# All of the down projection with the activations held in the array, the last norm in [tokens, columns], and shorter waits in the residual's turns

## The chip, the cores and the metric

The kernel runs on one core of one Trainium2 chip. The metric is the device time of one execution in microseconds (us); a kernel's time is the median of its runs. Three runs of the kernel before took 2245.82, 2247.30 and 2247.95 us.

## The reference

A decoder trunk in float32: 256 tokens, model width 2048, two layers (0 and 1). What it computes, cut to what matters here:

```python
for l in range(2):
    z = rmsnorm(x, attn_norm[l]) @ w_in[l]              # 2048 -> 4 head groups x (q, k, v) of 512
    x = x + concat(fox, moba, diff, stick_breaking)(z) @ w_out[l]
    h = rmsnorm(x, ffn_norm[l])
    act = silu(h @ w_gate[l]) * (h @ w_up[l])            # 2048 -> 5632
    x = x + act @ w_down[l]                              # 5632 -> 2048
return rmsnorm(x, final_norm)
# rmsnorm(x, g) = x / sqrt(mean(x * x over the 2048 columns) + 1e-6) * g
```

## The kernel before

**Number format.** Every weight is split on the chip into a rounded high half and the rest, a low half (hi and lo); activations are split in the same way. A product is the sum of three matmuls: hi by hi, hi by lo and lo by hi.

**Weights.** They come as blocks of 128 x 1024 float32 (512 KB) in the order of `plan()`. `run_ahead(b)` (L226) stands ahead of block b's matmuls: it issues the loads on SP's queue up to block b+5 (four raw buffers) and splits block b+2. Of a split, ACT makes hi (L199) and DVE makes lo (L200), into three pairs of buffers, so the split of block b+2 can't start before TensorE is through with block b-1. A load waits until its raw buffer's former block is split.

**Two forms of product.** `rows_block` (L360) holds the activations in the array (128 tokens) and streams 512 weight columns: 12 matmuls of 512 columns for a block, and the result is [tokens, columns]. `gate_up_product` (L377) does the same for gate and up. `product` (L414) holds the weights and streams the activations, so that the result is [columns, tokens]: for a block 8 matmuls of 512 columns and 8 of 256 (L431, L432), or, with `split_halves=False`, 24 matmuls of 256 columns (L435 to L437).

**The residual** `x_all` lies as [columns, tokens], 16 tiles `xs[j]` of 128 x 256. A result of `rows_block` has to be turned before it is added. `turn_steps` (L394) does that: two DVE transposes of 32x32 squares (L399), one DMA to DRAM (`mem`, L402), four DMAs back (`back`, L408). `add_turned` (L895) then adds `back` to four of the tiles with one DVE instruction (L899), and for each of the four makes the next product's halves `xh` (ACT L303, DVE L304) and the square (ACT L298), which POOL sums (L299).

**The order of the work** is written out by hand, and every engine runs its instructions in that order. Evacuations are generators in a FIFO queue, `evacs`. After each block's matmuls `tick()` takes one step of the oldest generator; a `yield` ends a step. A residual's turn has seven steps: transposes; `mem`; nothing; `back`; nothing; the add with two tiles' halves; two tiles' halves. So five splits are in the engines' queues between the transposes and the add.

**Where turns are added to the residual.** The output projection makes four groups of 512 columns, n = 0 to 3, in `OUT_ORDER`: n = 0 and 1 end two blocks apart, n = 2 and 3 take eight blocks each. So several of these turns follow one another in the FIFO queue without a free step. The down projection makes groups n = 0 to 2 with `rows_block` (22 blocks each, one turn each) and the last 512 columns as two groups of 256 with `product` (11 blocks each). In layer 0 both have hi and lo streamed together and are added by `add_to_x` (L874) without a turn. In layer 1 the last group goes straight to `final_norm` (L974).

**The end.** `final_norm` adds the last two tiles, sums the squares over partitions with matmuls against ones (L981), makes 1/sqrt with one Newton step, spreads it over partitions with a diagonal matmul (L324), scales the 16 tiles on DVE (L1007) and POOL (L1012), and stores `y_t` (2 MB) with ten DMAs. The final norm's gain is multiplied into each tile earlier.

Of the kernel before, what the change touches and what calls it, by code (L numbers as in the profile page):

```python
# [11 lines left out]
F32 = mybir.dt.float32  # L12
# [3 lines left out]
ALU = mybir.AluOpType  # L16
# [85 lines left out]
V_FIN = DEPTH * V_LAYER  # L102
V_ALL = V_FIN + 16


def lay_out(inp):
# [15 lines left out]
    for l in range(DEPTH):  # L122
        w_in, every = inp["w_in"][l][pd], slice(None)
        v = vec[:, l * V_LAYER:(l + 1) * V_LAYER]
        v[:, V_GA:V_GA + 16] = inp["attn_norm"][l][pd].reshape(16, P).T
        v[:, V_GF:V_GF + 16] = inp["ffn_norm"][l][pd].reshape(16, P).T
        v[:, V_WF:V_WF + 64] = w_in[:, FG0:FG0 + NH].reshape(16, P, NH).transpose(1, 0, 2).reshape(P, 64)
        v[:, V_SUB] = inp["diff_subln"][l]
        v[:, V_B:V_B + NH] = inp["b_fgate"][l]
        for n, name in enumerate(("diff_lq1", "diff_lk1", "diff_lq2", "diff_lk2")):  # L130
            v[:, V_LAM + 64 * n:V_LAM + 64 * (n + 1)] = inp[name][l]
        for kind, what, nb in plan():
            if what[0] != l:
                continue
            if kind == "in":
                put(w_in, every, columns(*what[1:]), GC)
            elif kind == "out":
                order = np.concatenate([HEAD0[g] * P + np.arange(GW) for g in ORDER])
                put(inp["w_out"][l], order[what[2] * 256:what[2] * 256 + 256], np.arange(what[1] * GC, what[1] * GC + GC), GC)
            elif kind == "ffn":  # L140
                c = slice(what[1] * GC, what[1] * GC + GC)
                for n, name in enumerate(("w_gate", "w_up")):
                    blocks[at:at + NJ, :, n * GC:n * GC + GC] = inp[name][l][:, c][pd].reshape(NJ, P, GC)
                at += NJ
            elif kind == "down":
                put(inp["w_down"][l], pf, slice(what[1] * GC, what[1] * GC + GC), GC)
            else:
                put(inp["w_down"][l], pf, pd[what[1] * 256:what[1] * 256 + 256], 256)
    vec[:, V_FIN:V_FIN + 16] = inp["final_norm"][pd].reshape(16, P).T
    return {"x_t": x_t, "vec": vec, "w": blocks, "consts": constants()}  # L150
# [7 lines left out]
def plan():  # L158

    out = []  # L160
    for l in range(DEPTH):
# [4 lines left out]
        out += [("down", (l, c), NFC * 2) for c in range(3)]  # L166
        out += [("last", (l, c), NFC) for c in (6, 7)]
# [4 lines left out]
def trunk(ctx: ExitStack, tc: tile.TileContext, x_t, vec, w, consts, y_t):  # L172
# [72 lines left out]
    def cst(at, n=P):  # L245
        return con[:, at:at + n]
# [69 lines left out]
    def diag_product(cols):  # L316

        diag = tp.tile([P, 2, P], F32, name="diag", tag="g", bufs=1)
        for t in range(2):
            V.tensor_scalar(diag[:, t], ident, cols[:, t:t + 1], None, op0=ALU.mult)  # L320
        yield
        pbc = ps.tile([P, 512], F32, name="pbc", tag="at")
        for t in range(2):
            T.matmul(pbc[:, t * P:(t + 1) * P], cst(C_ONE), diag[:, t], start=t == 0, stop=t == 1)  # L324
        return pbc

# [67 lines left out]
    def turn_steps(get, back=None):  # L394
# [8 lines left out]
        yield  # L403
        yield
# [5 lines left out]
        yield  # L410
        yield
        return back.rearrange("p a k n -> p k a n")

    def product(sources, n_b, tags=("mm",), order=None, split_halves=True, done=None):  # L414


        nonlocal block
        outs = [None] * len(tags)
        for n, kb in order or [(n, kb) for kb in range(n_b) for n in range(len(tags))]:
            if kb == 0:  # L420
                outs[n] = [ps.tile([P, 2 * S], F32, name=f"po{c}", tag=tags[n]) for c in range(2)]
            run_ahead(block)
            hi, lo = halves.pop(block)
            for kk in range(4):
                k = kb * 4 + kk
                xk = sources(k)
                for c in range(2):
                    at = kk * 256 + c * P
                    end = k == 4 * n_b - 1
                    if split_halves:  # L430
                        T.matmul(outs[n][c], hi[:, at:at + P], xk, start=k == 0, stop=False)  # L431
                        T.matmul(outs[n][c][:, S:], lo[:, at:at + P], xk[:, :S], start=False, stop=end)  # L432
                    else:
                        o = outs[n][c][:, :S]
                        T.matmul(o, hi[:, at:at + P], xk[:, S:], start=k == 0, stop=False)  # L435
                        T.matmul(o, lo[:, at:at + P], xk[:, :S], start=False, stop=False)
                        T.matmul(o, hi[:, at:at + P], xk[:, :S], start=False, stop=end)  # L437
            block += 1
            if done and kb == n_b - 1:
                done(n, outs[n])  # L440
            tick()
        return outs
# [431 lines left out]
    def add_to_x(c, po, gain):  # L874


        def use(j):
            if gain is not None:
                halves_of_x(j, gain(j))
            square_sum(j)  # L880
            if gain is None:
                A.activation(xs[j], xs[j], AF.Copy, scale=vecs[:, V_FIN + j:V_FIN + j + 1])

        for i in range(2):
            j = 2 * c + i
            t = tp.tile([P, S], F32, name="xt", tag="sq")
            V.tensor_tensor(t, xs[j], po[i][:, S:], op=ALU.add)
            V.tensor_tensor(xs[j], t, po[i][:, :S], op=ALU.add)
            if i:
                use(j - 1)  # L890
            yield
        use(2 * c + 1)
        yield

    def add_turned(n, outs, gain):  # L895

        new = yield from turn_steps(lambda t: outs[t])
        of = x_all[:, 4 * n:4 * n + 4].rearrange("p k (a n) -> p k a n", n=32)
        V.tensor_tensor(of, of, new, op=ALU.add)  # L899
        for j in range(4 * n, 4 * n + 4):  # L900
            if gain is not None:
                halves_of_x(j, gain(j))
            square_sum(j)
            if gain is None:
                A.activation(xs[j], xs[j], AF.Copy, scale=vecs[:, V_FIN + j:V_FIN + j + 1])
            if j % 2:
                yield

# [19 lines left out]
    def ffn(l):  # L928
# [24 lines left out]

        evacs.append(norm_steps("mm"))
        for c in range(NFC):
            evacs.append(act_steps(c, *gate_up_product(("at", "mm")[c % 2])))
        new_norm()
        xh.clear()
        last = l + 1 == DEPTH
        gain = None if last else lambda j: vcol(l + 1, V_GA + j)  # L960
        for n in range(3):
# [3 lines left out]
            evacs.append(add_turned(n, outs, gain))  # L965
        if last:
            A.activation(tp.tile([P, 1], F32, name="pre", tag="pre", bufs=1), cst(C_ONE, 1), AF.Sqrt)
        evacs.append(add_to_x(6, product(source, 11)[0], gain))
        if last:
            final_norm(product(source, 11, split_halves=False)[0])  # L970
        else:
            evacs.append(add_to_x(7, product(source, 11)[0], gain))

    def final_norm(po):  # L974

        drain(evacs)
        sums = ps.tile([P, 2], F32, name="sums_ps", tag="at")

        def add(sq, first, last):
            for t in range(2):  # L980
                T.matmul(sums[:, t:t + 1], sq[:, t * P:(t + 1) * P], cst(C_ONE, 1), start=first and t == 0,  # L981
                         stop=last and t == 1)

        add(state["acc"], True, False)
        for i in range(2):
            j = NJ - 2 + i
            V.tensor_tensor(xs[j], xs[j], po[i][:, :S], op=ALU.add)
            sq = tp.tile([P, S], F32, name="sq", tag="sq")
            A.activation(sq, xs[j], AF.Square)
            add(sq, False, i == 1)  # L990
        v = tp.tile([P, 2], F32, name="v", tag="nv")
        V.tensor_scalar(v, sums, 1.0 / D, EPS, op0=ALU.mult, op1=ALU.add)
        r = tp.tile([P, 2, 2], F32, name="rf", tag="rf", bufs=1)
        A.activation(r[:, 0], v, AF.Sqrt)
        for j in range(NJ - 2, NJ):
            A.activation(xs[j], xs[j], AF.Copy, scale=vecs[:, V_FIN + j:V_FIN + j + 1])
# [4 lines left out]
        pbc = finish(diag_product(r[:, 0]))  # L1001
        rbc = tp.tile([P, S], F32, name="rbc", tag="gt", bufs=1)
        A.activation(rbc, pbc[:, :S], AF.Copy)
        at = 0
        for n in (1, 1, 2, 2, 2, 2, 1, 1):
            for j in range(at, at + n):
                V.tensor_tensor(xs[j], xs[j], pbc[:, :S], op=ALU.mult)  # L1007
            nc.sync.dma_start(y_t[:, at:at + n], x_all[:, at:at + n])
            at += n
        for j in range(at, NJ, 2):  # L1010
            for i in range(2):
                G.tensor_tensor(xs[j + i], xs[j + i], rbc, op=ALU.mult)  # L1012
            nc.scalar.dma_start(y_t[:, j:j + 2], x_all[:, j:j + 2])
# [31 lines left out]
```

## Time and profile before

| | |
|---|---|
| median of three runs | 2247.3 us |
| the profiled execution | 2250.89 us |
| its span, first to last instruction | 2249.1 us |
| TensorE busy | 2227.5 us, 99% of the span |
| DVE busy | 1300.6 us, 58% |
| ACT busy | 1056.8 us, 47% |
| bytes moved | 473.31 MB, mean 210 GB/s |
| granted TensorE clock | 0.998 of 2.4 GHz |

Matmuls overlap their neighbours, so a busy share of TensorE near 100% doesn't say that it runs at its peak: the distance between the starts of two matmuls counts. A matmul's own duration in the rows is longer than that distance. Where a row has brackets, they hold the engine's idle time before the instruction and what ended it.

### The profile page before, as it was taken

The numbers are of one execution on the slowest core, as the hardware profiler recorded it, in microseconds if no ns is written. First come the engines' busy times: TensorE is split into PE (matmuls) and PEld (weight loads), VectorE is DVE, ScalarE is ACT, GpSimd is POOL, SyncE is SP. The second block draws the span as 40 slices with busy tenths as digits, with TensorE's granted clock in tenths as the row PEclk, the third lists the DMA queues.
The fourth block names the chain that finished last, engine by engine and source line by source line (L and its number), as shares of the span: only waits on it lengthen the run. The fifth ranks groups of instructions, "written<-read, shape, count | busy, mean of one in ns | idle before, by whom it ended". The sixth has DMA issues, their size and how long they took to land.

```text
span 2249.1 us, 27206 instructions
## 1 busy us (share of the span) xinstructions
PE 2227.5 (99%) x10257; PEld 1845.3 (82%) x10257; DVE 1300.6 (58%) x1450; ACT 1056.8 (47%) x1306; POOL 213.8 (10%) x206
## 2 busy tenths in 40 slices
PE   9999999999999999999999999999999999999998
PEld 6888887788888888888888888887888888888887
DVE  6768655655555555455566776566555555554444
ACT  6455644544444444444444555445444444444443
POOL 2019101100000000000000380011000000000001
PEclk9999999999999999999999999999999999999999
DMA  7766566776667667666657566576666766766674
GB/s 267 223 197 208 179 194 199 233 225 219 211 221 224 210 213 230 210 208 208 199 195 235 183 197 200 165 236 223 219 212 222 223 211 214 228 214 206 212 217 131
DMA packets 187491, 473.31 MB, mean 210 GB/s; under 512 B 17248, under 2 KB 71264, under 8 KB 187360
## 3 DMA queue, kind: packets, MB, share of 16 engines
q1 hardware_dynamic: 186928, 471.05, 65.7%
q8 instruction: 80, 1.31, 0.2%
q10 hardware_dynamic: 432, 0.53, 0.1%
q14 instruction: 51, 0.42, 0.0%
HBM read 442.16 MB, written 29.36 MB: 210 GB/s over the span
## 4 chain that ended last, share of the span: by engine, by line
PE 89%; DMA 4%; DVE 3%; ACT 1%; issue 1%; SPq 1%; DVEq 0%; ACTq 0%
PE gate L389 20%; PE up L389 20%; PE po L371 7%; PE po L373 7%; PE po L372 7%; PE in L371 7%; PE in L372 7%; PE in L373 7%; PE po L431 3%; DMA back<-mem 2%; PE po L432 1%; DVE lo L200 1%; DMA mem<-tr 1%; ACT hi L199 1%; DMA raw<-w 1%
## 5 line engine op out<-in xcount | busy, mean ns | idle before, releaser
L200 DVE TENSOR_TENSOR lo<-raw,hi 128x1024 fp32r<-128x1024 f32 (+1 forms) x785 | 962.9, 1229 | 886.5 <-ACT hi L199 886.2
L199 ACT ACTIVATE hi<-raw 128x1024 fp32r<-128x1024 f32 (+1 forms) x785 | 829.9, 1059 | 1078.5 <-PE up L389 494.5
L389 PE MATMUL gate<-hi,xh 128*128 128x512 f32 x1408 | 548.4, 389 | 0.9 <-ACT hi L199 0.9
L389 PE MATMUL up<-hi,xh 128*128 128x512 f32 x1408 | 548.3, 389 | 0.0
L389 PEld LDWEIGHTS gate<-hi,xh 128*128 128x128 f32 x1408 | 264.5, 188 | 56.4 <-ACT hi L199 1.8
L389 PEld LDWEIGHTS up<-hi,xh 128*128 128x128 f32 x1408 | 264.3, 188 | 54.9
L371 PE MATMUL in<-hi,xh 128*128 128x512 f32 x768 | 303.4, 395 | 1.0 <-ACT hi L199 1.0
L372 PE MATMUL in<-lo,xh 128*128 128x512 f32 x768 | 300.0, 391 | 2.1 <-DVE lo L200 2.1
L373 PE MATMUL in<-hi,xh 128*128 128x512 f32 x768 | 299.5, 390 | 0.0
L389 PE MATMUL gate<-lo,xh 128*128 128x512 f32 x704 | 274.6, 390 | 1.1 <-DVE lo L200 1.1
L389 PE MATMUL up<-lo,xh 128*128 128x512 f32 x704 | 274.2, 389 | 0.0
L299 POOL TENSOR_TENSOR acc<-acc,sq 128x256 f32<-128x256 f32 x73 | 67.9, 930 | 1726.0 <-ACT sq L298 1723.2
L371 PE MATMUL po<-hi,act 128*128 128x512 f32 x528 | 205.5, 389 | 0.0
L373 PE MATMUL po<-hi,act 128*128 128x512 f32 x528 | 205.5, 389 | 0.0
L372 PE MATMUL po<-lo,act 128*128 128x512 f32 x528 | 205.5, 389 | 0.0
L372 PEld LDWEIGHTS in<-lo,xh 128*128 128x128 f32 x768 | 144.5, 188 | 33.3 <-DVE lo L200 4.6
L371 PEld LDWEIGHTS in<-hi,xh 128*128 128x128 f32 x768 | 144.4, 188 | 31.1 <-ACT hi L199 2.3
L373 PEld LDWEIGHTS in<-hi,xh 128*128 128x128 f32 x768 | 144.3, 188 | 30.4
L389 PEld LDWEIGHTS gate<-lo,xh 128*128 128x128 f32 x704 | 132.2, 188 | 30.3 <-DVE lo L200 3.2
L389 PEld LDWEIGHTS up<-lo,xh 128*128 128x128 f32 x704 | 132.1, 188 | 27.3
L373 PEld LDWEIGHTS po<-hi,act 128*128 128x128 f32 x528 | 99.1, 188 | 20.7
L372 PEld LDWEIGHTS po<-lo,act 128*128 128x128 f32 x528 | 99.1, 188 | 20.5
(218 smaller groups left out, 1920.7 us busy)
## 6 DMA issues: line engine op xcount, KB each, us to landing
raw<-w SPq DMA_DIRECT2D x783, 512.0 KB, 4.2
mem<-tr SPq DMA_DIRECT2D x52, 512.0 KB, 4.2
back<-mem SPq DMA_DIRECT2D x176, 128.0 KB, 5.2
k<-mem SPq DMA_DIRECT2D x24, 128.0 KB, 5.0
x_all<-x_t SPq DMA_DIRECT2D x7, 256.0 KB, 6.5
q<-mem SPq DMA_DIRECT2D x8, 128.0 KB, 3.9
y_t<-x_all SPq DMA_DIRECT2D x4, 256.0 KB, 3.0
raw<-w SPq DMA_DIRECT2D x2, 256.0 KB, 3.7
```

The lines of the kernel that those rows point to most:

```text
L199: A.activation(hi[:, c], raw[:, c], AF.Copy)
L200: V.tensor_tensor(lo[:, c], raw[:, c], hi[:, c].bitcast(F32), op=ALU.subtract)
L299: G.tensor_tensor(state["acc"], state["acc"], sq, op=ALU.add)
L371: T.matmul(outs[t], xlo, wh, start=first, stop=False)
L372: T.matmul(outs[t], xhi, wl, start=False, stop=False)
L373: T.matmul(outs[t], xhi, wh, start=False, stop=last)
L389: T.matmul(outs[n][t], st, wt[:, n * GC:(n + 1) * GC], start=first, stop=last)
L431: T.matmul(outs[n][c], hi[:, at:at + P], xk, start=k == 0, stop=False)
L432: T.matmul(outs[n][c][:, S:], lo[:, at:at + P], xk[:, :S], start=False, stop=end)
```

## The change

- `turn_steps` gets a parameter `wait`: the free steps after `mem` and again after `back`. It stays at 2 for the q, k and activation turns. `add_turned` passes 1, so a residual's turn has five steps: transposes; `mem`; `back`; the add with two tiles' halves; two tiles' halves.
- `down` has four groups of 512 columns, all with `rows_block`; `product` and `add_to_x` go. In layer 0 the fourth group is turned and added like the others, while layer 1's first input product runs.
- In layer 1 the residual is turned to [tokens, columns] once, ahead of down: `row_steps`, four of them, each after the activation turn of chunks 2 to 5 of gate and up. Down's four groups are then added without a turn (`last_steps`), squares are summed along the columns by ACT, and the final norm's gain comes as four tiles of 128 x 512 loaded from `fin`.
- `final_norm` has no matmuls; the result is stored as `y` [128, 2, 2048] with eight DMAs of 256 KB.

```diff
@@ plan
-        out += [("down", (l, c), NFC * 2) for c in range(3)]
-        out += [("last", (l, c), NFC) for c in (6, 7)]
+        out += [("down", (l, c), NFC * 2) for c in range(4)]
@@ turn_steps
-    def turn_steps(get, back=None):
+    def turn_steps(get, back=None, wait=2):
         ...
         nc.sync.dma_start(mem.rearrange("t i r g n -> (i r) t (g n)"), tr)
-        yield
-        yield
+        for _ in range(wait):
+            yield
         ...
         for g in range(4):
             nc.sync.dma_start(back[32 * g:32 * g + 32].rearrange("r a k n -> r a (k n)"),
                               mem[:, :, :, g].rearrange("t i r n -> r (t i) n"))
-        yield
-        yield
+        for _ in range(wait):
+            yield
         return back.rearrange("p a k n -> p k a n")
@@ add_turned
-        new = yield from turn_steps(lambda t: outs[t])
+        new = yield from turn_steps(lambda t: outs[t], wait=1)
@@ new
+    def row(n):
+        return x_all[:, 4 * n:4 * n + 4].rearrange("p k s -> p (k s)").rearrange("p (t c) -> p t c", t=2)
+
+    def row_steps(n):
+        c = tp.tile([P, 8, 4, 32], F32, name="c", tag="back", bufs=1)
+        A.activation(c, x_all[:, 4 * n:4 * n + 4].rearrange("p k (a n) -> p a k n", n=32), AF.Copy)
+        yield
+        tr = tp.tile([P, 8, P], F32, name="trb", tag="tr", bufs=1)
+        for t in range(2):
+            V.transpose(tr[:, 4 * t:4 * t + 4].rearrange("p a n -> p (a n)"),
+                        c[:, 4 * t:4 * t + 4].rearrange("p a k n -> p (a k n)"))
+        yield
+        mem = dr.tile([8, 32, 4, P], F32, name="memb", tag="mem")
+        for g in range(4):
+            nc.sync.dma_start(mem[:, :, g].rearrange("a c n -> c a n"), tr[32 * g:32 * g + 32])
+        yield
+        yield
+        nc.sync.dma_start(row(n), mem.rearrange("(t i) c g n -> (i c) t (g n)", t=2))
+        yield
@@ ffn
         for c in range(NFC):
             evacs.append(act_steps(c, *gate_up_product(("at", "mm")[c % 2])))
+            if last and 2 <= c < 6:
+                evacs.append(row_steps(c - 2))
         ...
-        for n in range(3):
+        for n in range(4):
             outs = [ps.tile([P, GC], F32, name=f"po{t}", tag="mm") for t in range(2)]
             for kb in range(NF // 2):
                 rows_block(source, outs, kb, NF // 2)
-            evacs.append(add_turned(n, outs, gain))
+                if last and kb == 4:
+                    gains[n] = big.tile([P, GC], F32, name=f"fin{n}", tag=f"xh{n}")
+                    nc.sync.dma_start(gains[n], fin[:, n * GC:n * GC + GC])
+            if not last:
+                evacs.append(add_turned(n, outs, lambda j: vcol(l + 1, V_GA + j)))
+            elif n < 3:
+                evacs.append(last_steps(n, outs, ssq, gains[n]))
         if last:
+            final_norm(outs, ssq, gains[3])
-            A.activation(tp.tile([P, 1], F32, name="pre", tag="pre", bufs=1), cst(C_ONE, 1), AF.Sqrt)
-        evacs.append(add_to_x(6, product(source, 11)[0], gain))
-        if last:
-            final_norm(product(source, 11, split_halves=False)[0])
-        else:
-            evacs.append(add_to_x(7, product(source, 11)[0], gain))
+    def last_steps(n, outs, ssq, gain):
+        x = row(n)
+        for t in range(2):
+            V.tensor_tensor(x[:, t], x[:, t], outs[t], op=ALU.add)
+        yield
+        junk = tp.tile([P, 2, GC], F32, name="junk", tag="tr", bufs=1)
+        for t in range(2):
+            A.activation(junk[:, t], x[:, t], AF.Square, accum_out=ssq[:, t, n:n + 1])
+        yield
+        V.tensor_tensor(x, x, gain[:, None, :].to_broadcast([P, 2, GC]), op=ALU.mult)
+        if n == 2:
+            A.activation(tp.tile([P, 1], F32, name="pre", tag="pre", bufs=1), cst(C_ONE, 1), AF.Sqrt)
+        yield
@@ final_norm (its new body)
+        drain(evacs)
+        x = row(3)
+        ...
+        for t in range(2):
+            V.tensor_tensor(x[:, t], x[:, t], outs[t], op=ALU.add)
+            A.activation(junk[:, t], x[:, t], AF.Square, accum_out=ssq[:, t, 3:4])
+        end = tp.tile([P, 2, GC], F32, name="end", tag="g", bufs=1)
+        V.tensor_tensor(end[:, 0], x[:, 0], gain, op=ALU.mult)
+        v = tp.tile([P, 2], F32, name="v", tag="nv")
+        V.tensor_reduce(v, ssq, axis=AX, op=ALU.add)
+        V.tensor_scalar(v, v, 1.0 / D, EPS, op0=ALU.mult, op1=ALU.add)
         ...
+        for n in range(4):
+            x = row(n) if n < 3 else end
+            for t in range(2):
+                to = y[:, t, n * GC:n * GC + GC]
+                if n == 3 and t == 1:
+                    V.scalar_tensor_tensor(end[:, t], row(3)[:, t], r[:, 0, t:t + 1], gain, op0=ALU.mult, op1=ALU.mult)
+                    nc.sync.dma_start(to, x[:, t])
+                elif t == 0 or n == 3:
+                    V.tensor_scalar(x[:, t], x[:, t], r[:, 0, t:t + 1], None, op0=ALU.mult)
+                    nc.sync.dma_start(to, x[:, t])
+                else:
+                    A.activation(x[:, t], x[:, t], AF.Copy, scale=r[:, 0, t:t + 1])
+                    nc.scalar.dma_start(to, x[:, t])
```

## Rows read from the trace of the kernel before

**Rows 1.** The page's part 1: engine, busy us (share of the span), instructions.

```profile
PE 2227.5 (99%) x10257; PEld 1845.3 (82%) x10257; DVE 1300.6 (58%) x1450; ACT 1056.8 (47%) x1306; POOL 213.8 (10%) x206
```

**Rows 2.** Windows: from:to length, then PE, PEld, DVE, ACT, POOL, clock, DMA.

```profile
1060.87:1123.04 62.17, 62.17 (x354) 53.96 (x352) 34.88 (x35) 27.46 (x34) 5.42 (x6) 1.00 0.64 203
1993.09:2172.61 179.52, 179.52 (x794) 148.72 (x792) 89.24 (x78) 79.92 (x88) 6.51 (x7) 1.00 0.66 211
2172.61:2203.69 31.08, 31.08 (x178) 26.97 (x176) 15.84 (x14) 14.77 (x20) 3.61 (x4) 1.00 0.74 218
2203.69:2235.37 31.68, 31.68 (x267) 31.68 (x266) 12.69 (x14) 11.16 (x13) 2.88 (x2) 1.00 0.32 104
2235.53:2249.10 13.57, 2.61 (x16) 2.15 (x15) 5.81 (x21) 2.22 (x6) 2.78 (x4) 0.62 0.43 155
```

**Rows 3.** Waits: who waited for whom, us in total, times, longest.

```profile
DVE x_all L899 <- DMA back<-mem: 12.0, 7, 2.6
...
SPq L408 <- DMA mem<-tr: 24.2, 29, 2.2
```

**Rows 4.** Timeline, DVE then SP, layer 0's first down turn (start, length).

```profile
943.63 1.31 DVE L399 STREAM_TRANSPOSE tr<-po 128x512 f32<-128x512 f32 x2
...
950.64 1.23 DVE L200 TENSOR_TENSOR lo<-raw,hi 128x1024 fp32r<-128x1024 f32 x1 [1.50 <-ACT hi L199]
...
957.23 1.22 DVE L899 TENSOR_TENSOR x_all<-x_all,back 128x1024 f32<-128x1024 f32 x1
...
944.96 0.38 SPq L402 DMA_DIRECT2D mem<-tr  x1
946.46 3.05 SPq L190 DMA_DIRECT2D raw<-w  x2
949.89 1.80 SPq L408 DMA_DIRECT2D back<-mem  x4
```

**Rows 5.** Timeline, DVE, output projection's turn n = 1 in layer 0.

```profile
373.27 1.30 DVE L399 STREAM_TRANSPOSE tr<-po 128x512 f32<-128x512 f32 x2
...
377.91 1.23 DVE L200 TENSOR_TENSOR lo<-raw,hi 128x1024 fp32r<-128x1024 f32 x1 [1.10 <-ACT hi L199]
...
387.05 1.23 DVE L899 TENSOR_TENSOR x_all<-x_all,back 128x1024 f32<-128x1024 f32 x1 [2.47 <-DMA back<-mem]
```

**Rows 6.** Timeline, DVE then PE, around turn n = 3's add.

```profile
414.40 1.30 DVE L399 STREAM_TRANSPOSE tr<-po 128x512 f32<-128x512 f32 x2
...
427.30 1.23 DVE L899 TENSOR_TENSOR x_all<-x_all,back 128x1024 f32<-128x1024 f32 x1 [2.36 <-DMA back<-mem]
...
430.35 0.39 PE L389 MATMUL up<-hi,xh 128*128 128x512 f32 x1
431.08 0.50 PE L389 MATMUL gate<-hi,xh 128*128 128x512 f32 x1 [0.34 <-ACT hi L199]
...
432.34 0.50 PE L389 MATMUL gate<-lo,xh 128*128 128x512 f32 x1 [0.53 <-DVE lo L200]
```

**Rows 7.** Source lines L402, then L408, all turns: issue of one DMA to landing.

```profile
DMA to landing us min/median/max: 3.4/4.2/6.8
...
DMA to landing us min/median/max: 3.1/5.1/7.4
```

**Rows 8.** Instructions by line: busy us, mean ns of one, idle before.

```profile
L943 ACT ACTIVATE act<-back 128x512 fp32r<-128x512 f32 x44 | 27.4, 622 | 12.4 <-DMA back<-mem 12.2
...
L543 DVE TENSOR_TENSOR mix<-po,mix 128x512 fp32r<-128x512 f32 x12 | 8.0, 678 | 1.1 <-ACT mix L542 1.1
```

**Rows 9.** The chain of waits at the end: start, length, what.

```profile
2238.24 0.17 DVE rf L1000
...
2240.45 0.42 DVE x_all L1007
```

**Rows 10.** DMA rate in 40 slices of the tail, 2235.5 to 2249.1.

```profile
GB/s 0 0 0 0 0 0 0 0 0 0 0 0 0 0 0 0 0 0 193 235 319 277 386 373 392 356 392 386 386 386 386 368 392 322 341 283 0 0 0 0
```

**Rows 11.** Window after the clock's fall at the end (columns as in rows 2).

```profile
2238.70:2249.10 10.40, 1.22 (x4) 0.93 (x4) 4.28 (x14) 0.38 (x1) 2.78 (x4) 0.50 0.56 202
```

More of the change, by code (lines that the diff above doesn't have):

```diff
@@ L101 @@
 V_LAYER = V_LAM + 4 * 64
-V_FIN = DEPTH * V_LAYER
-V_ALL = V_FIN + 16
+V_ALL = DEPTH * V_LAYER
 def lay_out(inp):
@@ L144, in lay_out @@
                 at += NJ
-            elif kind == "down":
+            else:
                 put(inp["w_down"][l], pf, slice(what[1] * GC, what[1] * GC + GC), GC)
-            else:
-                put(inp["w_down"][l], pf, pd[what[1] * 256:what[1] * 256 + 256], 256)
-    vec[:, V_FIN:V_FIN + 16] = inp["final_norm"][pd].reshape(16, P).T
-    return {"x_t": x_t, "vec": vec, "w": blocks, "consts": constants()}
+    fin = np.ascontiguousarray(np.broadcast_to(inp["final_norm"], (P, D)))
+    return {"x_t": x_t, "vec": vec, "w": blocks, "consts": constants(), "fin": fin}
 OUT_ORDER = [(c, kb) for c in range(2) for kb in range(6)] + [(c, kb) for c in range(2) for kb in range(6, 8)]
@@ L165, in plan, with trunk @@
         out += [("ffn", (l, c), NJ) for c in range(NFC)]
-        out += [("down", (l, c), NFC * 2) for c in range(3)]
-        out += [("last", (l, c), NFC) for c in (6, 7)]
+        out += [("down", (l, c), NFC * 2) for c in range(4)]
     return out
 @with_exitstack
-def trunk(ctx: ExitStack, tc: tile.TileContext, x_t, vec, w, consts, y_t):
+def trunk(ctx: ExitStack, tc: tile.TileContext, x_t, vec, w, consts, fin, y):
     nc = tc.nc
@@ L314, in inv_sqrt @@
         V.tensor_tensor(out, t[:, 0, :n], t[:, 1, :n], op=ALU.mult)
[L316 to L320, printed above, removed]
-        yield
[L322 to L325, printed above, removed]
     def norm_steps(tag="at"):
@@ L409, in turn_steps @@
                               mem[:, :, :, g].rearrange("t i r n -> r (t i) n"))
-        yield
-        yield
+        for _ in range(wait):
+            yield
         return back.rearrange("p a k n -> p k a n")
[L414 to L442, printed above, removed]
     heads = {}
@@ L872, in group_steps @@
         yield from STEPS[name](l, *(by_heads(name, which, qk[which]) for which in "qk"), ready)
[L874 to L893, printed above, removed]
     def add_turned(n, outs, gain):
-        new = yield from turn_steps(lambda t: outs[t])
+        new = yield from turn_steps(lambda t: outs[t], wait=1)
         of = x_all[:, 4 * n:4 * n + 4].rearrange("p k (a n) -> p k a n", n=32)
@@ L900, in add_turned @@
         for j in range(4 * n, 4 * n + 4):
-            if gain is not None:
-                halves_of_x(j, gain(j))
+            halves_of_x(j, gain(j))
             square_sum(j)
-            if gain is None:
-                A.activation(xs[j], xs[j], AF.Copy, scale=vecs[:, V_FIN + j:V_FIN + j + 1])
             if j % 2:
                 yield
+    def row(n):
[16 more added lines that the diff above has]
+        yield
     def out_projection(l):
@@ L952, in source @@
             return act[k]
+        last = l + 1 == DEPTH
         evacs.append(norm_steps("mm"))
@@ L956, in ffn @@
             evacs.append(act_steps(c, *gate_up_product(("at", "mm")[c % 2])))
+            if last and 2 <= c < 6:
+                evacs.append(row_steps(c - 2))
         new_norm()
         xh.clear()
-        last = l + 1 == DEPTH
-        gain = None if last else lambda j: vcol(l + 1, V_GA + j)
-        for n in range(3):
+        ssq = tp.tile([P, 2, 4], F32, name="ssq", tag="isq")
+        gains = {}
+        for n in range(4):
             outs = [ps.tile([P, GC], F32, name=f"po{t}", tag="mm") for t in range(2)]
@@ L964, in ffn @@
                 rows_block(source, outs, kb, NF // 2)
-            evacs.append(add_turned(n, outs, gain))
-        if last:
-            A.activation(tp.tile([P, 1], F32, name="pre", tag="pre", bufs=1), cst(C_ONE, 1), AF.Sqrt)
-        evacs.append(add_to_x(6, product(source, 11)[0], gain))
-        if last:
-            final_norm(product(source, 11, split_halves=False)[0])
-        else:
-            evacs.append(add_to_x(7, product(source, 11)[0], gain))
-    def final_norm(po):
-        drain(evacs)
[L977 to L990, printed above, removed]
+                if last and kb == 4:
+                    gains[n] = big.tile([P, GC], F32, name=f"fin{n}", tag=f"xh{n}")
+                    nc.sync.dma_start(gains[n], fin[:, n * GC:n * GC + GC])
@@ L991, in final_norm @@
+    def final_norm(outs, ssq, gain):
+        drain(evacs)
+        x = row(3)
+        junk = tp.tile([P, 2, GC], F32, name="junk", tag="tr", bufs=1)
+        for t in range(2):
[3 more added lines that the diff above has]
+        V.tensor_tensor(end[:, 0], x[:, 0], gain, op=ALU.mult)
         v = tp.tile([P, 2], F32, name="v", tag="nv")
-        V.tensor_scalar(v, sums, 1.0 / D, EPS, op0=ALU.mult, op1=ALU.add)
+        V.tensor_reduce(v, ssq, axis=AX, op=ALU.add)
+        V.tensor_scalar(v, v, 1.0 / D, EPS, op0=ALU.mult, op1=ALU.add)
@@ L993, in final_norm @@
         r = tp.tile([P, 2, 2], F32, name="rf", tag="rf", bufs=1)
         A.activation(r[:, 0], v, AF.Sqrt)
-        for j in range(NJ - 2, NJ):
-            A.activation(xs[j], xs[j], AF.Copy, scale=vecs[:, V_FIN + j:V_FIN + j + 1])
         V.reciprocal(r[:, 0], r[:, 0])
@@ L1000, in final_norm @@
         V.scalar_tensor_tensor(r[:, 0], r[:, 1], 1.5, r[:, 0], op0=ALU.add, op1=ALU.mult)
[L1001 to L1013, printed above, removed]
+        for n in range(4):
[8 more added lines that the diff above has]
+                    nc.sync.dma_start(to, x[:, t])
+                else:
+                    A.activation(x[:, t], x[:, t], AF.Copy, scale=r[:, 0, t:t + 1])
+                    nc.scalar.dma_start(to, x[:, t])
     zero = tp.tile([P, 2 * S], BF16, name="zero", tag="g", bufs=1)
@@ L1036 @@
     args = [nc.dram_tensor(n, a.shape, F32, kind="ExternalInput").ap() for n, a in arrays.items()]
-    y = nc.dram_tensor("y_t", (P, NJ, S), F32, kind="ExternalOutput").ap()
+    y = nc.dram_tensor("y", (P, 2, D), F32, kind="ExternalOutput").ap()
     with tile.TileContext(nc) as tc:
@@ L1040 @@
     r = run_bass_kernel_spmd(nc, [arrays], core_ids=[0])
-    got = r.results[0]["y_t"]
-    out = np.empty((S, D), np.float32)
-    out[:, turned(D)] = got.transpose(1, 0, 2).reshape(D, S).T
+    out = np.ascontiguousarray(r.results[0]["y"].transpose(1, 0, 2).reshape(S, D))
     return out[None]
```

## The prediction, on record before the changed kernel ran

> **What bounds the kernel now.** I read the engine shares first, then the stretches of the down projection and the tail, then the waits, and last the timelines of three residual turns. TensorE is busy 99% of the span, DVE 58%, ACT 47% [rows 1]: the time is the sum of TensorE's start-to-start distances, plus what it waits, plus the tail. In down the forms differ in that distance. 792 matmuls of 512 columns take 179.52 us, 226.7 ns each; the `product` form takes 353 ns for a pair of 512 and 256 columns (176 pairs in layer 0, 88 in layer 1); 264 matmuls of 256 columns take 31.68 us, 120.0 ns each [rows 2]. So 256 more columns cost 106.7 ns, and every matmul carries about 13.3 ns besides its columns. The tail, from the last matmul to the end, is 13.57 us [rows 2].
>
> The waits show who is near to holding TensorE up. DVE's add of a residual turn waits for the DMAs back in 7 of 14 turns, 12.0 us together, 2.6 at most; SP waits for `mem` to land in 29 turns [rows 3]. What such a wait does is in the third timeline: DVE's add waits 2.36 us, everything behind it on DVE and ACT waits too, and TensorE stops for a hi and then for a lo [rows 6].
>
> **Part 1: down with activations held.** Columns and loads don't change, the count of matmuls does: a block has 12 instead of 16 or 24. 22 blocks of the new form take 22 x 12 x 0.2267 = 59.85 us. They replace 62.17 us in layer 0 (gain 2.32) and 31.08 + 31.68 = 62.76 in layer 1 (gain 2.91) [rows 2]. TensorE is full there, so this counts: **-5.2 us**. Below 4.5 or above 5.5 it can hardly be, since both forms are in the trace. Weighed against this: the Trainium skill, "TensorE: Matmul & The Clock Gate", section "Back-to-back issue gap", gives columns over 2.4 GHz plus 2.5 ns for a warm matmul. By that the estimated gain is 0.7 us (33 blocks save 10 ns, 11 save 31), and the sum below would be 4.5 us higher. The rows have 13.3 ns instead of 2.5.
>
> **Part 2: turns with one block of waiting.** All 12 remaining residual turns change: four in each output projection, four in layer 0's down. DVE takes its instructions in order. Between the transposes and the add there were five splits, now there are three. Nothing in the round trip gets shorter by that: `mem` goes out when the transposes end (944.94 to 944.96), `back` when `mem` has landed, and the add reads what came back.
>
> Supply: after a turn that starts with DVE up to date, the third lo ends at 950.64 + 1.23 = 951.87, 6.9 us after the transposes' end [rows 4]. Demand: `mem` 4.2 us (3.4 at least), the four `back` issues 1.4 from first to last, the last one's landing some 4.0, between its least of 3.1 and its median of 5.1, as one raw load less stands ahead of it [rows 4, 7]. Together 9.6 us; the ends are 7.9 from the two least values and 11.6 from turn n = 3, whose add started 427.30 - 415.70 after its transposes [rows 6]. So DVE idles 9.6 - 6.9 = 2.7 us in each such turn, where five splits covered it (957.23, without a wait).
>
> Price: queued behind the add are, on ACT, two halves and two squares and the next hi, on DVE two halves and the next lo; TensorE has blocks for 2 x 2.72 us, less what is used up. The one measured case fixes it: wait 2.36; the next product matmul was due at 430.58 and the third one, the first to need lo, at 431.03; it started at 432.34, with 0.1 us more in slow matmuls [rows 6]. Price: the wait less 0.95 us. Eight turns start with DVE up to date (n = 0 and 3 of each output projection, the four of down): 8 x 1.7 = 13.6 us.
>
> n = 1 and 2 of each output projection follow straight on another turn, before as after, because the FIFO has no free step there. Their transposes come late against the splits, which then catch up: the third lo ends at 377.91 + 1.23 = 379.14, only 4.6 us after the transposes' end at 374.57 [rows 5]. Wait 9.6 - 4.6 = 5.0, stall 4.05, times four = 16.2 us. n = 3 is of the adjacent kind before; after, three ticks are free ahead of it.
>
> Stalls that are there already go, since they are replaced: 12.0 us in six long waits and a short one, 11.8 - 6 x 0.95 = 6.1 us [rows 3]. Net of part 2: 13.6 + 16.2 - 6.1 = **+23.7 us**. Ends: round trip 7.9, 0 + 4 x 2.35 - 6.1 = +3.3; 11.6, 8 x 3.75 + 4 x 6.05 - 6.1 = +48.
>
> SP's queue: `back` moves ahead of one raw load, which then goes out some 2.5 us later (the second of the two at 946.46 would leave after the four `back`, 1.80 us). It is wanted four blocks, 10.9 us, after it normally goes out, and lands in about 5, so 3 us of cover stay: 0. On the layer boundary the fourth turn now stands between down and the input product, which first wants its tiles in its seventh block, 16.3 us on; they are there at about 3.8 + 9.6 + 2.3 = 15.7. With `wait=2` that would have been late; with 1 it is one of the eight stalls.
>
> **Part 3: the last layer's turn and norm.** The four `row_steps` (an ACT copy of 1024 columns, two transposes, five DMAs) and the three `last_steps` lie beside full TensorE stretches in which ACT and DVE have about half their time free [rows 1, 2], in free steps of the FIFO (an activation turn takes 8 of 16 ticks, `row_steps` 5). Cost 0; if one of their DMAs is late, SP holds raw loads behind it, and each wait beyond 3 us would show: up to +4 together.
>
> The end: after the last matmul an add of 512 columns (0.68), a square (0.62 and its sum's readout, 0.2) [rows 8], a reduce, and the same small steps as now from `v` to the corrected root, 0.2 each: the root is there about 3.2 us after the last matmul, as now (2238.41 less 2235.5 = 2.9) [rows 9]. But the first scaled tile now comes 2.0 us later, at 2240.45, after the diagonal matmul, its copy and the waits between them; this goes. Then scale 0.5, first packets 0.65 later, as now, 2 MB at about 380 GB/s [rows 10], the rate that bounds the stores, 5.5, and 1.2 to the end: 11.05 instead of 13.57: **-2.5 us**, between 0 (the eight stores queue badly) and -4.
>
> **Sum.** -5.2 + 23.7 - 2.5 + 0 = +16.0 us. The profiled execution took 2250.9 us, 1.8 more than its span of 2249.1 and 3.6 above the median; it becomes 2266.9, and the median of runs 2247.3 + 16.0 = **2263 us**. Less than 4.5 us either way, 0.2%, can't be told from no change.
>
> **Rivals.**
> *The round trip is shorter than it looks* (faster). The waits of before hide the true length: fewer raw loads are in flight, TensorE's stops thin out the loads, and both landings come near their least. At 7.9 us the eight turns stall 0.05 each and the four 2.35, net +3.3; with the other parts -4.4: 2243 us. For it: `mem` did land in 3.4 and a `back` in 3.1 [rows 7]. Against: those are least values of 52 and 208, and both in each of 12 turns is much to ask. It decides at a round trip of 8.3 us: below that the kernel is faster. The Trainium skill, "DMA: Bandwidth & Descriptors", section "Anatomy of one DMA — SWDGE (gpsimd) path", has 2.0 us plus bytes over 436 GB/s, for DMAs that GpSimd issues: an estimate of 3.2 for `mem`, 2.3 for a `back`, 6.9 in all, and a time near 2239. The medians here are 4.2 and 5.1. Chance 0.18.
>
> *The clock falls in the long stalls* (slower still). After 2238.7 the granted clock is 0.50 (the 1.2 GHz level), TensorE's last product matmul having been at 2235.4 [rows 2, 11]: about 3 us with next to no work. The four long stalls come near that. Each fall would add one to two blocks at half speed, 2.7 to 5.4 us: four give +11 to +22, 2274 to 2285. Chance 0.17.
>
> *The stall isn't paid*: the three split blocks cover it, in these turns and the old ones; then only -5.2 - 2.5 and the 6.1 remain: 2233.5. Against it stands the measured case [rows 6]. Chance 0.05.
>
> *The matmul form brings nothing*: the 13.3 ns go with the operands and not with each matmul; part 1 is then 0 and the time 2268. Against it, the 66 blocks ahead of layer 1's last groups run in the new form, on the same operands, at 226.7 ns [rows 2]. Chance 0.03.
>
> **How the numbers follow.** Forecast 0.57, with its own range of 2250 to 2278. Faster by over 0.2% (below 2242.8): the third rival, two thirds of the first and a sliver of the forecast, 0.18. Within 0.2%: the rest of the first and the forecast's low end, 0.07. Slower: 0.75. The range reaches from the short round trip to the fallen clock: 2243 to 2283.
>
> **What would show it.** Right: DVE's add waits in all 12 turns, about 2.7 us in eight and 5 in four, 40 us together instead of 12.0; TensorE idle on hi and lo after each; down's last 512 columns in 59.85 us; no L324 at the end, the tail near 11 us. Wrong: an add's waits of 15 us or less in total, a TensorE stall well under the wait less 0.95, or raw loads that come late because SP stood behind `mem`.

## The result, and the profile after

The changed kernel is slower: 2275.08 us, median of four runs (2272.54 to 2279.96), against 2247.62 us. The ratio is 1.0122, interval 1.0100 to 1.0145. Run again twice beside other kernels it was 1.0096 (1.0081 to 1.0112) and 1.0090 (1.0074 to 1.0106). The profiled execution took 2279.96 us, its span is 2278.1 us; it is the slowest of the four, and the sums below go against the profiled execution of before (2250.89, span 2249.1): +29.0 us of span.

The engines' shares have hardly moved [rows 1]. The page's part 1 of the changed kernel:

```profile
PE 2234.9 (98%) x9977; PEld 1836.6 (81%) x9977; DVE 1304.0 (57%) x1442; ACT 1053.8 (46%) x1296; POOL 196.9 (9%) x189
```

Two parts of the change did what was forecast. Windows of the changed kernel, columns as in [rows 2]; the first is layer 1's whole down, the second the tail:

```profile
2027.35:2266.48 239.13, 239.13 (x1057) 198.01 (x1055) 116.41 (x102) 98.62 (x104) 0.00 (x0) 1.00 0.61 191
2266.87:2278.10 11.23, 0.00 (x0) 0.00 (x0) 4.63 (x14) 3.77 (x8) 0.00 (x0) 0.65 0.50 187
```

1056 matmuls in 239.13 us are 226.5 ns each, the pace of [rows 2], so layer 1's last 22 blocks take 59.8 us instead of 62.8. Layer 0's take as long in the new form, where no add waits: in the run a_wait2 below, its third and fourth add start 59.84 us apart; before it was 62.2. The tail takes 11.23 instead of 13.57 us [rows 2]. The root is ready 2.9 us after the last matmul, and the first scaled tile starts with it, where before it came 2.0 us later [rows 9]. The tail's timeline on DVE (the last small step, the first scalings, the last one) and the first store:

```profile
2269.60 0.16 DVE L964 SCALAR_TENSOR_TENSOR rf<-rf 128x2 f32<-128x2 f32 x1
...
2269.80 1.28 DVE L973 TENSOR_SCALAR x_all<-x_all,rf 128x512 f32<-128x512 f32 x3
2270.31 1.42 SPq L974 DMA_DIRECT2D y<-x_all  x3
...
2271.39 0.74 DVE L970 SCALAR_TENSOR_TENSOR end<-x_all,rf,fin 128x512 f32<-128x512 f32 x1
```

The shorter waits, part 2 of the prediction, cost more than both give. Waits of the changed kernel (who waited for whom, us, times, longest), where L833 is the add, L299 the halves on ACT and, from SP's own waits, L393 the loads back:

```profile
ACT xh L299 <- DVE x_all L833: 72.4, 12, 8.3
DVE x_all L833 <- DMA back<-mem: 42.2, 12, 5.7
```

```profile
SPq L393 <- DMA mem<-tr: 46.3, 31, 3.2
```

Every one of the 12 adds now waits for its DMAs, 42.2 us together, against 7 of 14 and 12.0 us [rows 3]. SP, too, stands longer for `mem`, 46.3 us instead of 24.2, with raw loads queued behind it. That isn't what costs: ACT's hi waits for a raw load 2.8 us in all, no longer than before, and in none of the three stretches that hold the 12 turns. First the kernel before, then the changed one:

```profile
ACT hi L199 <- DMA raw<-w: 4.1, 5, 1.7
```

```profile
ACT hi L195 <- DMA raw<-w: 2.8, 4, 1.2
```

DVE's timeline of layer 0's first down turn shows how the add comes to wait; it answers to [rows 4]:

```profile
954.58 1.31 DVE L384 STREAM_TRANSPOSE tr<-po 128x512 f32<-128x512 f32 x2
956.16 1.23 DVE L196 TENSOR_TENSOR lo<-raw,hi 128x1024 fp32r<-128x1024 f32 x1 [0.27 <-ACT hi L195]
958.88 1.23 DVE L196 TENSOR_TENSOR lo<-raw,hi 128x1024 fp32r<-128x1024 f32 x1 [1.49 <-ACT hi L195]
961.60 1.23 DVE L196 TENSOR_TENSOR lo<-raw,hi 128x1024 fp32r<-128x1024 f32 x1 [1.50 <-ACT hi L195]
965.55 1.23 DVE L833 TENSOR_TENSOR x_all<-x_all,back 128x1024 f32<-128x1024 f32 x1 [2.73 <-DMA back<-mem]
967.36 0.48 DVE L300 SCALAR_TENSOR_TENSOR xh<-x_all,vecs,xh 128x256 fp32r<-128x256 f32 x1 [0.58 <-ACT xh L299]
...
969.32 1.23 DVE L196 TENSOR_TENSOR lo<-raw,hi 128x1024 fp32r<-128x1024 f32 x1 [0.77 <-ACT hi L195]
```

Three splits instead of five stand between the transposes and the add, and DVE stands idle for 2.73 us with the next lo queued behind it. The DMAs take about as long as before: the landings of `mem` (L387) and then of `back` (L393), which answer to [rows 7], have a median of 4.4 us each, instead of 4.2 and 5.1.

```profile
DMA to landing us min/median/max: 3.5/4.4/7.2
...
DMA to landing us min/median/max: 2.4/4.4/7.3
```

In the output projection's second turn of layer 0 (it answers to [rows 5]) DVE stands idle for 5.31 us. First DVE there, then SP, then TensorE at the block that had to wait:

```profile
369.52 1.30 DVE L384 STREAM_TRANSPOSE tr<-po 128x512 f32<-128x512 f32 x2
...
373.57 1.22 DVE L196 TENSOR_TENSOR lo<-raw,hi 128x1024 fp32r<-128x1024 f32 x1 [0.50 <-ACT hi L195]
380.10 1.23 DVE L833 TENSOR_TENSOR x_all<-x_all,back 128x1024 f32<-128x1024 f32 x1 [5.31 <-DMA back<-mem]
```

```profile
370.85 0.38 SPq L387 DMA_DIRECT2D mem<-tr  x1
...
375.09 1.80 SPq L393 DMA_DIRECT2D back<-mem  x4
```

```profile
380.21 0.39 PE L358 MATMUL po<-hi,mix 128*128 128x512 f32 x1
383.88 0.80 PE L356 MATMUL po<-hi,mix 128*128 128x512 f32 x1 [3.28 <-ACT hi L195]
385.14 0.80 PE L357 MATMUL po<-lo,mix 128*128 128x512 f32 x1 [0.46 <-DVE lo L196]
385.73 0.63 PE L358 MATMUL po<-hi,mix 128*128 128x512 f32 x1
386.16 0.63 PE L356 MATMUL po<-hi,mix 128*128 128x512 f32 x1
```

TensorE stands for a hi, then for a lo, as in [rows 6], and then its matmuls start 0.43 us apart instead of 0.23: the granted clock has fallen to its lower level, 1.2 GHz. Windows of the two falls in this place; the clock is the number before the last two:

```profile
382.60:389.40 6.80, 5.06 (x11) 3.69 (x12) 6.26 (x8) 4.54 (x8) 3.02 (x4) 0.50 0.31 94
403.10:409.90 6.80, 6.10 (x14) 4.79 (x15) 4.67 (x5) 3.70 (x6) 1.81 (x2) 0.50 0.54 175
```

It fell four more times ahead of the tail, for 3.4 us each (at 1096.0, 1498.7, 1536.3 and 1563.6), every time in a stall of this kind or right behind one. So six of the 12 adds were followed by a fall, and six weren't.

I add up TensorE's excess, the distance between starts beyond 226.7 ns a matmul of 512 columns, from 6 us before to 13 us after each add. It is 7.6 us before and 44.9 after; 33.2 of the 44.9 are waits and 11.7 matmuls slowed by the lower clock. So 44.9 - 7.6 - 5.2 - 2.3 = +29.8 us, against +29.0 of span.

### The profile page after: what moved, and what is told of

Read it like the earlier page. It is cut to its first block, busy times and chain, and to the rows that moved or that the text cites. A ratio compares the mean times of both kernels' runs of the same rounds, so it can differ in the third digit from the quotient of the medians.

```text
span 2278.1 us, 26623 instructions
## 1 busy us (share of the span) xinstructions
PE 2234.9 (98%) x9977; PEld 1836.6 (81%) x9977; DVE 1304.0 (57%) x1442; ACT 1053.8 (46%) x1296; POOL 196.9 (9%) x189
## 4 chain that ended last, share of the span: by engine, by line
PE 88%; DMA 4%; DVE 3%; ACT 2%; issue 1%; SPq 1%; ACTq 0%; DVEq 0%
PE gate L374 21%; PE up L374 21%; PE po L357 8%; PE po L358 8%; PE po L356 8%; PE in L357 7%; PE in L356 7%; PE in L358 7%; DMA mem<-tr 2%; DVE lo L196 1%; DMA raw<-w 1%; ACT hi L195 1%; DMA back<-mem 1%; SPq L393 1%; DVE tr L384 1%
## 5 line engine op out<-in xcount | busy, mean ns | idle before, releaser
L357 PE MATMUL po<-lo,act 128*128 128x512 f32 x704 | 275.2, 391 | 2.3 <-DVE lo L196 2.3
L356 PE MATMUL po<-hi,act 128*128 128x512 f32 x704 | 274.8, 390 | 2.6 <-ACT hi L195 2.6
L358 PE MATMUL po<-hi,act 128*128 128x512 f32 x704 | 274.6, 390 | 0.0
L356 PEld LDWEIGHTS po<-hi,act 128*128 128x128 f32 x704 | 132.6, 188 | 31.6 <-ACT hi L195 3.9
L357 PEld LDWEIGHTS po<-lo,act 128*128 128x128 f32 x704 | 132.4, 188 | 31.2 <-DVE lo L196 3.8
L358 PEld LDWEIGHTS po<-hi,act 128*128 128x128 f32 x704 | 132.6, 188 | 27.4
```

The source lines that it names most:

```text
L356: T.matmul(outs[t], xlo, wh, start=first, stop=False)
L357: T.matmul(outs[t], xhi, wl, start=False, stop=False)
L358: T.matmul(outs[t], xhi, wh, start=False, stop=last)
```

## The experiments

Theory W: the shorter wait makes DVE stand at the add until the DMAs are back, and TensorE pays. Rivals: the new product form or the new norm costs the time (F); or what hurts is that the add's work comes earlier in the queues, not that it waits (W2). All ratios are against the kernel before, run beside it.

**Two blocks of waiting again, all else changed (a_wait2).**

```diff
-        new = yield from turn_steps(lambda t: outs[t], wait=1)
+        new = yield from turn_steps(lambda t: outs[t], wait=2)
```

> The changed kernel with two blocks of waiting again in the residual's turns; the down form and the last norm stay changed. Theory W (the shorter waits make DVE and ACT stand before the add, and TensorE stalls and its clock falls): the changed kernel's trace has 44.9 us of TensorE excess after the 12 adds against 7.6 before, so 37.3 go. 2275.1 less 37.3 gives 2238, plus 0 to 2.5 for layer 0's fourth turn, whose halves are then wanted about 2 us before they are there: 2238 to 2242. Rival F (the down form, or the new norm, cost the time): stays above 2260.

Measured: 2248.55 us, ratio 0.9996 (0.9987 to 1.0006). F is out: with the old waits the slowdown is gone, and the adds wait as they did before:

```profile
DVE x_all L833 <- DMA back<-mem: 10.4, 6, 3.0
```

The number missed by 7 us. One reason is in the expectation: it took the excess of the slowest execution off the median of all. Another is that the kernel before took 1.9 us more beside this run than in the first result. The third is the layer boundary, where the fourth turn's halves were late as forecast; TensorE's timeline there:

```profile
1137.54 0.39 PE L358 MATMUL in<-hi,xh 128*128 128x512 f32 x1
1139.81 0.50 PE L356 MATMUL in<-hi,xh 128*128 128x512 f32 x1 [1.89 <-DVE xh L300]
```

That cost 3.9 us with the fall of the clock behind it; the adjacent turns keep their old stalls. Excess in all 11.5 us, 3.9 above that of before, so only 3 to 4 us of the 7.5 would stay by this profile (its span is 2245.0), and the medians show 0.9 (between 2.9 gained and 1.3 lost).

**The waits alone, on the kernel before (b_only_wait).** `turn_steps` gets the parameter as in the change, and

```diff
-        new = yield from turn_steps(lambda t: outs[t])
+        new = yield from turn_steps(lambda t: outs[t], wait=1)
```

> The kernel before with one thing changed: its residual turns wait one block at each step. Fourteen turns are concerned, three of them in layer 1's down. Theory W: eight turns of the output projections cost what they cost in the changed kernel (34.6 us of excess, clock included), six turns of down some 2.2 to 4 each (13 to 20), and the 7.6 of before go: 2288 to 2296. Rival F: within 3 us of 2247.6.

Measured: 2281.49 us, ratio 1.0143 (1.0122 to 1.0165), 32 us slower. The shorter wait alone does it. This is more than the changed kernel's 27.5 us because parts 1 and 3 aren't there to give 7.5 back; the turns themselves don't cost more. All 14 adds wait, among them the three of layer 1's down, and TensorE's excess after them is some 36 us:

```profile
DVE x_all L899 <- DMA back<-mem: 39.9, 14, 6.1
```

It stayed under the expected 2288: the six down turns had 1.3 to 2.4 us of wait and cost some 10 us in all, where 13 to 20 were expected, and the eight turns of the output projections cost some 27 instead of 34.6.

**One block of the two given back (c_wait12).** The first number of the pair is the free steps after the store to `mem`, the second those after the loads into `back`.

```diff
-        for _ in range(wait):
+        for _ in range(waits[0]):
...
-        for _ in range(wait):
+        for _ in range(waits[1]):
...
-        new = yield from turn_steps(lambda t: outs[t], wait=1)
+        new = yield from turn_steps(lambda t: outs[t], waits=(1, 2))
```

> The changed kernel with one free step after the store to DRAM and two after the loads back, so four splits between transposes and add. Theory W: every wait of an add shrinks by one block, 2.72 us. The isolated ones (2.1 to 3.1 us in the changed kernel) go to 0 to 0.4 and stall nothing; the adjacent ones (3.4 to 5.7) keep 1 to 3 us and cost up to 2 each, without a fall of the clock; adds wait 10 to 16 us in all. 2275.1 less 33 to 38: 2237 to 2242. A rival W2, that it is the early place of the add's work in the queues and not the DMA's landing that stalls: still two thirds of the excess, about 2260.

Measured: 2253.04 us, ratio 1.0008 (0.9998 to 1.0018), 11 us above the expectation. The time alone decides nothing: it lies between what W and W2 expected. The waits speak for W. The six turns that stood alone, the first of each output projection and the four of down, wait no more. But the waits that stay are longer than thought:

```profile
DVE x_all L833 <- DMA back<-mem: 16.4, 6, 4.7
```

With six steps instead of five the fourth turn of the output projection again follows straight on the third: its adds waited 4.1 and 4.7 us, the excess was 4.2 and 5.4 with the clock's fall. I had counted its steps for five.

**No trip through DRAM (d_no_trip).** The same five steps, the add at the same place, but it reads the transposed tile; what it leaves out stands in the expectation.

```diff
-        new = yield from turn_steps(lambda t: outs[t], wait=1)
+        tr = tp.tile([P, 2, GC], F32, name="tr", tag="tr", bufs=1)
+        for t in range(2):
+            V.transpose(tr[:, t], outs[t])
+        yield
+        yield
+        yield
+        new = tr.rearrange("p t c -> p (t c)").rearrange("p (a k n) -> p k a n", a=8, k=4)
```

> The changed kernel, its residual turns in the same five steps, but without the trip through DRAM: the add reads the transposed tile itself, in the order in which it lies there, so the residual gets the right sums at the wrong places. It leaves out 12 stores and 48 loads. Theory W: with nothing to wait for, the add's wait is 0 in all 12 turns, no stall after any, the clock never falls before the end: 2275.1 - 44.9 = about 2230, 2228 to 2234. Rival W2 (the place of the add's work in the queues): the stalls stay, 2255 or more.

Measured: 2235.83 us, ratio 0.9941 (0.9926 to 0.9956), 1.8 us above the expected range (2228 to 2234). No add waits for a DMA, TensorE's excess after the 12 adds is 0.0, and the clock stays up to the tail. ACT's halves wait for the add 29.1 us instead of 72.4, 2.4 at most instead of 8.3:

```profile
ACT xh L299 <- DVE x_all L839: 29.1, 12, 2.4
```

W2 is out: the work in its early place is free. Nor is it the raw loads that gain from the 60 DMAs left out: hi waits for them 2.3 us here and 2.8 in the changed kernel. The profiled execution took 2235.09 us, 44.9 less than the changed kernel's profiled one. That this is the excess to 0.1 us is partly luck, since the changed kernel's four executions lie up to 7.4 us apart; by the medians the two kernels differ by 39 us, by the ratios by 41.

**Does the lower clock cost anything by itself? (e_fill, e_fill3).** Matmuls that nobody reads stand ahead of the block that will stall, so that TensorE isn't idle. `fill` issues `fills.pop(block, 0)` matmuls of 512 columns, `con_r` by `con_r`; `gate_up_product` calls it in the same place. `n_fill` is 12 for n = 1 and 2 of the output projection and 4 elsewhere (3 in e_fill3).

```diff
     def rows_block(source, outs, kb, n_b):
...
         run_ahead(block)
+        fill("at")
         hi, lo = halves.pop(block)
...
         V.tensor_tensor(of, of, new, op=ALU.add)
+        fills[block + 2] = n_fill
```

> The changed kernel with matmuls that nobody reads put ahead of the block that stalls after each of the 12 adds: 12 of 512 columns (2.7 us) in the four turns that follow straight on another, 4 (0.9 us) in the other eight. They run while TensorE would have waited for hi, so the stall itself stays as long. Theory C (the clock's falls are a cost of their own on top of the waits: 11.7 us of slow matmuls in the profiled execution): the clock stays at 1.00 through the turns, and the time falls by 7 to 11 us against the changed kernel's run beside it. Rival: the slow matmuls run in time that would be waited anyway; then the time stays within 2 us or rises by the extra matmuls that find no wait, up to 3 us.

Measured: 2271.69 us, ratio 1.0102 (1.0088 to 1.0116); the changed kernel beside it (after_again, below) 2271.87 us, 1.0096. The fillers did their work: the slow matmuls' share of the excess fell from 9.1 us (after_again) to 1.7. In 11 of the 12 places TensorE still waited after them, so they took next to no time themselves. The time did not fall. With fewer fillers, after which TensorE still waited in all 12 places:

> As with the fillers of 12 and 4 matmuls, now 12 and 3, so that fewer find no wait. Theory C (a fall of the clock costs 1.6 us, at four to six falls 6 to 9 us): the waits as in the changed kernel, the clock at 1.00 through nearly all turns, and the median 4 us or more below the changed kernel's beside it. Rival: the falls cost next to nothing in time, since the slow matmuls lie where TensorE would soon wait again: medians within 2 us, as in the first try.

Measured: 2271.92 us, 1.0091 (1.0077 to 1.0106), beside it the changed kernel (after_five) 2271.36 us, 1.0090. The expectation for the changed kernel beside it,

> The changed kernel with more rounds, to be compared with the next one: 1.0 to 1.2% above the kernel before. In its profile the adds wait 38 to 43 us and the clock falls four to six times ahead of the tail.

held in the ratio and in the falls, four, but not in the waits, which were 36.6 us. Theory C's 4 us and more isn't seen: the medians of the two pairs differ by -0.2 and +0.6 us, and together the executions' scatter leaves some 3 us either way. So the falls cost less than about 3 us on balance. One reason can be seen between the second and third add of layer 1's output projection, first in the changed kernel (after_five, clock 0.83 in the window 1508 to 1528), then with fillers (e_fill3, 1.00 in it):

```profile
1508.85 1.23 DVE L833 TENSOR_TENSOR x_all<-x_all,back 128x1024 f32<-128x1024 f32 x1 [4.92 <-DMA back<-mem]
1527.18 1.23 DVE L833 TENSOR_TENSOR x_all<-x_all,back 128x1024 f32<-128x1024 f32 x1 [3.07 <-DMA back<-mem]
```

```profile
1510.41 1.23 DVE L845 TENSOR_TENSOR x_all<-x_all,back 128x1024 f32<-128x1024 f32 x1 [4.80 <-DMA back<-mem]
1528.82 1.23 DVE L845 TENSOR_TENSOR x_all<-x_all,back 128x1024 f32<-128x1024 f32 x1 [5.32 <-DMA back<-mem]
```

```profile
1508.00:1528.00 20.00, 16.63 (x61) 12.86 (x60) 12.14 (x13) 7.90 (x13) 3.31 (x4) 0.83 0.64 210
```

```profile
1508.00:1528.00 20.00, 19.18 (x83) 15.09 (x82) 11.25 (x12) 7.91 (x13) 3.35 (x4) 1.00 0.68 212
```

From add to add it is 18.33 us with the low clock and 18.41 without. In the other traces of these kernels it is 18.42 with a fall between the two adds (after_again), and 18.85 (the changed kernel's first trace) and 18.21 (e_fill) without. Adjacent turns are a chain of their own: add, halves, transposes, store, loads, next add, longer than the five blocks (13.6 us) beside it. With a slower TensorE the next add only waits less for its DMAs (3.07 instead of 5.32 us). Ahead of the fourth turn, which stands alone, a fall isn't repaid: from the third add to the fourth it is 24.5 to 26.7 us in the changed kernel's three traces (six places, a fall in each) and 23.8 to 24.8 with fillers (four places, no fall), 1.4 us apart on average. Two such places in an execution make some 3 us, which the medians can't tell from nothing.

The same kernel beside e_fill (after_again):

> The changed kernel once more, beside the next two on one chip. All theories: 1.0 to 1.4% above the kernel before.

Measured 2271.87 us, 1.0096 (1.0081 to 1.0112), at the low end of what was expected.

**Free steps by turn (f_tuned).** The changed kernel, with `wait` as a pair, after `mem` and after `back`; the first of the two calls is the output projection's, the second layer 0's down:

```diff
-        new = yield from turn_steps(lambda t: outs[t], wait=1)
+        new = yield from turn_steps(lambda t: outs[t], waits=waits)
...
-                evacs.append(add_turned(n, outs[n], lambda j: vcol(l, V_GF + j)))
+                evacs.append(add_turned(n, outs[n], lambda j: vcol(l, V_GF + j), (2, 3) if n % 2 else (2, 2)))
...
-                evacs.append(add_turned(n, outs, lambda j: vcol(l + 1, V_GA + j)))
+                evacs.append(add_turned(n, outs, lambda j: vcol(l + 1, V_GA + j), (2, 2) if n < 3 else (1, 2)))
```

> The changed kernel with free steps chosen by turn: 2 and 2 in general; 2 and 3 for the output projection's second and fourth turn, whose adds waited 1.0 to 3.0 us with 2 and 2; 1 and 2 for layer 0's fourth down turn, whose halves were 2.05 us late with 2 and 2 and whose add waited 2.6 us with 1 and 1. Theory W: adds wait under 3 us in all, the stalls of 7.6 us before go but for some 0.7, no fall of the clock: 5.2 + 2.3 + 6.9 = 14.4 us under the kernel before, ratio 0.9936. Rival: the stall only moves on to the next turn (the longer second turn pushes the fourth into the first chunk of gate and up, whose thirteenth block wants its tiles): within 4 us of the kernel before.

Measured: 2236.64 us, ratio 0.9948 (0.9936 to 0.9961), 12.5 us under the kernel before, 1.9 short of what was expected, and faster than both kernels. Four adds still wait:

```profile
DVE x_all L833 <- DMA back<-mem: 2.3, 4, 1.3
```

Excess after the adds is 1.1 us instead of 7.6 before. So 6.5 of the 12.5 us come from the turns, which leaves 6.0 for the down form and the norm, where the windows have 7.5; the interval is 5.6 us wide and holds both. The profiled execution (2238.97 us) also has a fall of the clock near the start, from 11.3 us and 6.8 long, which has nothing to do with the turns.

## Why the prediction was right

Forecast 2263 us, measured 2275.1; slower was the likeliest case, for the reason given, and the size was 27.5 us instead of 16.

- *Part 1* was to bring 5.2 us: 59.8 us for 22 blocks, as summed. *Part 3* was to bring 2.5 us and brought 2.3; `last_steps` cost nothing (239.13 us for layer 1's down is the bare pace), nor did `row_steps`: from 1580 to 2020 us, where they lie, TensorE's matmuls start 226.7 ns apart throughout.
- *Part 2, the supply and the demand*: a round trip of 9.6 us was taken between 7.9 and 11.6. Measured from the transposes' end to the last landing it was 8.9 to 10.9 in the 12 turns, 9.6 on average. The adds were to wait about 40 us, and waited 42.2.
- *The price*, wait less 0.95 us, was a little low. Without the clock's share the eight single turns cost 17.5 us where 13.6 stood in the sum, the four adjacent ones 15.7 where 16.2 stood. Waits of 42.2 us and stalls of 33.2 make it 0.75 us a turn that isn't paid. The stalls of before were 7.6 where 6.1 were taken off.
- *The clock* is the term that the sum held at 0. It was a rival, with 11 to 22 us and a chance of 0.17, for falls after the four long stalls. It fell six times, after three of the four long stalls and after three single turns, and 11.7 us of slow matmuls stand in the profile, 2 us a fall where the rival had 2.7 to 5.4. The rival's price was wrong in kind as well: it was added on top of the waits, and with the falls taken away the time stayed within some 3 us. Falls between adjacent turns are paid back, since the next add then waits less; those ahead of the fourth turn aren't.
- *What is left*: the excess grew by 37.3 us where the sum had 23.7: 1.9 more from waits (33.2 less 7.6, instead of 29.8 less 6.1) and 11.7 from the clock. These 13.6 us cover the profiled execution's +29.1 against +16.0. The medians differ less (27.5, later 22.7 and 21.9), and the profiled execution was the slowest of its four. The fillers' runs had longer waits than the changed kernel beside them (41.4 and 41.9 us against 38.6 and 36.6). So what the clock is worth of the 6 to 12 us by which the forecast was too low stays open; how the waits vary from run to run (36.6 to 42.2 us in three profiles of the changed kernel) was not tested.
- *The rivals for faster* fell by their own rows: the round trip never came to 8.3 us, and no stall was covered by the three split blocks.

The Trainium skill's gap formula ("TensorE: Matmul & The Clock Gate", "Back-to-back issue gap") would have made part 1 worth 0.7 us; the 226.5 ns measured speak for the 5.2.

## What to carry to other kernels

A step that only waits in a schedule written by hand can be a landing's cover: before removing it, compare the time from the last producer to the landing with the time until the engine gets to the reader, turn by turn, because turns that follow straight on one another start late and have less cover. An engine that takes its instructions in order pays such a wait for all that is queued behind it, even when it is idle 40% of the time. Where one turn sits tight at a boundary, as layer 0's fourth down turn here, shorten that one alone.

## What the runs showed of the hardware

- The clock fell after short stops, but not after each. With the old waits TensorE stood 1.89 us in one piece at layer 1's start, and 0.7 us later the clock went to 0.50 for 3.4 us. In the changed kernel it fell after stops of 1.12 and 0.76 us (up to 1093.9 and 1095.2), and stayed up after stops of 2.25 and 0.76 us (up to 1516.4 and 1517.7).
- A lower clock isn't always time lost: between the same two adds it took 18.33 us with it and 18.41 without.
